# Hybrid GLA / state-space trunk: how the state-space preparation is stored, loaded and ranked

## The chip, the core and the metric

The kernel runs on one core of a Trainium2 chip. The metric is the device time of one execution in microseconds (us), the median of several runs. Engines are named as in the profile: PE is the matrix engine (PEld its weight loads), DVE the vector engine, ACT the scalar engine, POOL GpSimd, SP the engine from whose queue most transfers are issued.

## What is computed

A sequence of 512 tokens of width 1024 goes through two layers and a final norm. Layer 0 is gated linear attention with four heads, layer 1 a state-space mixer with 128 groups of 64 complex states:

```python
for i in range(DEPTH):                        # DEPTH = 2
    if i % 2 == 0:
        h = _rmsnorm(x, gla_norm[j])
        out = _gla_mixer(h, gla_w_in[j], gla_w_gate_up[j], gla_b_gate[j], gla_head_gain[j], gla_w_out[j])
    else:
        h = _rmsnorm(x, s5_norm[j])
        out = _s5_mixer(h, s5_w_in[j], s5_lam_re[j], s5_lam_im[j], s5_log_dt[j], s5_b_re[j], s5_b_im[j],
                        s5_c_re[j], s5_c_im[j], s5_d[j], s5_w_glu[j], s5_b_glu[j], s5_w_out[j])
    x = x + out
return _rmsnorm(x, final_norm)

# in _s5_mixer: what depends on parameters alone
dt = jnp.exp(log_dt)[:, None]
lam_bar = jnp.exp(lam * dt)
b_bar = ((lam_bar - 1.0) / lam)[..., None] * b_cplx
# and the recurrence that it is needed for: state <- lam_bar * state + b_bar u, y = Re(C state) + d u
```

## The kernel before, in words

The program is unrolled. Every instruction is traced in program order, and a scheduler then writes a fixed order for each engine ahead of time: it simulates the engines, and whenever one is free it takes, of the instructions whose inputs are there, the one with the lowest priority number. That number counts up with each traced instruction. `later(n)` adds n to it for a block, so that the block ranks as if it had been traced n instructions later. On the chip each engine then works through its written order, and an instruction whose input is late holds up all that stand behind it on that engine.

Layer 0 runs head by head (h = 0 to 3). A head projects v (`proj_v`), q and k (`proj_qk`) and z (`proj_z`), does the attention in four token blocks (`Attn.scores`, `state`, `mix`), and turns its output by PE transposes (`turn`). The output projection of a head (`proj_out`) is run inside the next head, between `proj_v` and `proj_z`. Weights come in units of 128 x 1024 (`wunit`): one load to `wraw` from SP's queue (L175), a cast to a high half on ACT (L158 or L180), and the low half by a DVE subtraction (L159) or by an accumulating transfer from POOL's queue (L181, L182). A matmul takes three passes, high by high, high by low, low by high. `proj_v` leaves its result in the four PSUM banks `pd`, and its evacuation `ev` (ACT L161, DVE L162) has to empty them before `proj_out` can use them.

The state-space layer needs matrices that depend on parameters alone. `S5Prep` builds them beside layer 0. Its `small` part is a generator in steps, one for a `tick()` in head 0: exponentials, sines, powers of lam_bar. Its fourth step makes the powers on POOL, its fifth transposes them on PE and stores them: `lpt` in 16 transfers of 32 KB (L1221), `pw` in four (L1224). `zero()` stores zero pads in `kz`, with 16 transfers of 56 KB from one tile (L957); it is called after head 0's `weave`. From head 1 on, `hook()` takes steps from a list, `plan`, at a rate (`RATES`) for each unit of the main work:

- F, for 16 blocks: `finish_b` of the block before, `compute` (eleven DVE operations, L1283 to L1301), `load` of the next block (four transfers, L1267 to L1273). The first F also loads block 0.
- Z: `finish_z`, which stores the rest, makes a convolution kernel on PE, and writes it to `kz`.
- E, for 8 tables: `etab`, six forms of DVE operation on 512 columns, twelve operations for two tables (L1251 to L1256), and four stores of 256 KB each (L1259). Its input `et` is made on POOL in the third step of `small`.
- G: `gcopy`, a rearranging copy.

`LOWS` gives what `later` adds for each kind of step. The first entries of `plan` are F0, E0, E1, F1, Z1, E2. All steps carry `issue_after(mark[...])`: they stand behind the last weight unit on each engine. The pools that matter here are `q4` (9 buffers of 4 KB a partition) and `tmp` (4 buffers of 2 KB).

The lines that the change and the prediction touch:

Of the kernel before, what the change touches and what calls it, by code (L numbers as in the profile page):

```python
# [9 lines left out]
F32 = mybir.dt.float32  # L10
# [11 lines left out]
P = 128  # L22
# [37 lines left out]
USP = 50  # L60
SEQ0 = 'h0 u h2 u h4 u s h6 u x0 t x1 q0 q1 t'
GP = 4
RATES = [0.84, 0.84, 0.88, 0.94, 0.94]
LOWS = {'F': 30, 'Z': 30, 'E': 100, 'G': 0}
ETABS = [2, 3, 3, 3, 3, 3, 3, 3, 4, 4, 4, 4, 4, 4, 4, 7, 8]
POS = [[0, 0, 1, 2, 1, 2, 3, 1, 2, 3, 3], [0, 1, 1, 3, 4, 5, 6, 5, 5, 7, 9], [0, 1, 3, 4, 4, 5, 6, 5, 6, 8, 8], [1,
    1, 4, 4, 4, 5, 6, 6, 6, 6, 8], [0, 0, 0, 0]]
# [20 lines left out]
def trunk_kernel(  # L88
# [5 lines left out]
    nc = tc.nc  # L94
    V, A, G, S, PE = nc.vector, nc.scalar, nc.gpsimd, nc.sync, nc.tensor
# [19 lines left out]
    def PT():  # L115
        return PS_("pt", 2)
# [19 lines left out]
    def tmp(dt=F32):  # L136
        return T_([P, 512], "tmp", 4, dt)
# [16 lines left out]
    mark = {}  # L154
# [169 lines left out]
    prep = S5Prep(tc, dr, C_, T_, PT, ident, q4, q2, big, tmp, s_bi, s_xc)  # L324
# [4 lines left out]
    @contextmanager  # L329
    def later(n):  # L330
        tc.cur_priority += n
        yield
        tc.cur_priority -= n

    def pinned(fn):
        with ExitStack() as es_:
            for k in ("pe", "act", "dve", "sp"):
                es_.enter_context(tc.issue_after(mark[k]))
            fn()

    def tick():
        if prep.t in SMALL:
            with later(LOW1):
                pinned(lambda: next(sm, None))
        prep.t += 1

    plan = []
    ne = 0
    for cb in range(NB + 1):
        plan.append(("F", cb))  # L350
        if cb:
# [8 lines left out]
    def hook():  # L360
        pace[0] += RATES[phase[0]]
        while pace[0] >= 1:
            pace[0] -= 1
            if plan:
                st = plan.pop(0)
                with later(LOWS[st[0]]):
                    prep.step(mark, *st)
# [41 lines left out]
    def proj_r():  # L409
        raw = tmp()[:, :P].rearrange("p (k n) -> p k n", n=16)  # L410
        hi = tmp(F32R)[:, :P].rearrange("p (k n) -> p k n", n=16)
        lo = tmp(F32R)[:, :P].rearrange("p (k n) -> p k n", n=16)
        S.dma_start(out=raw, in_=w_r.rearrange("p (k n) -> p k n", n=16))
        split(hi, lo, raw)
        acc = PT()
        for kb in range(8):
            three(acc[:16, :], hi[:, kb, :], lo[:, kb, :], hh[kb], hl[kb], kb == 0, kb == 7, True)
        V.tensor_tensor(out=rT, in0=acc[:16, :], in1=rbc[:16, :], op=MUL)
# [116 lines left out]
    def weave(gens, toks):  # L535
        i = 0
        for gen in gens:
            for _ in gen:
                with later(SCP):
                    for p, fn, b in toks:  # L540
                        if p == i:
                            fn(b)
                if prep.t < TOFF:
                    if i % 2:
                        tick()
                else:
                    hook()
                i += 1
# [79 lines left out]
    for h in range(NH):  # L628
        v = ([], [])
        box = []  # L630
        o = ([], [])
        trn = turn(box, o)
        if h == 0:
            v = v0
            proj_r()
        phase[0] = h - 1 if h else 0
        gt = nxt.pop() if nxt else gate(h)
        if h > 0:
            ptrn(0)
            ptrn(1)  # L640
        qk = proj_qk(h, gt[1], gt[2])
        if h > 0:
            ptrn(2)
            ptrn(3)
        if h == 0:
            tick()
        else:
            for _ in range(QZ[0]):
                hook()
        at_ = Attn(gt[0], qk, v, box)  # L650
        z = proj_z(h, box)
        tk = toks(h, at_)
        if h < 3 and GP >> h & 1:
            tk.append((GPOS[h], lambda b: nxt.append(gate(b)), h + 1))
        if h == 0:
            weave([z], tk)
            prep.zero()
            tick()
        elif h < NH - 1:
            weave([proj_v(h, *v), proj_out(h - 1, prev, range(2)), z], tk)  # L660
        else:
            weave([proj_v(h, *v), proj_out(h - 1, prev, range(1)), z], tk)
            weave([proj_out(h - 1, prev, (1,))], [(POS[4][b], trn, b) for b in range(4)])
            load_a(0)
            load_b(0)
        prev, ptrn = o, trn
# [20 lines left out]
    pt = PT()  # L687
# [194 lines left out]
    w = win()  # L882
# [22 lines left out]
    for tb in range(NT):  # L905
        for k in range(2):
            S.dma_start(out=f(x1p)[k * 64:(k + 1) * 64, 2 * tb:2 * tb + 2].rearrange("p q d -> p (q d)"),
                        in_=x1d.rearrange("(c j) d -> j c d", j=T)[2 * tb + k])
# [21 lines left out]
class S5Prep:  # L930
# [21 lines left out]
    def zero(self):  # L952
        zero = self.tmp()[:, :112]
        self.nc.gpsimd.memset(zero, 0.0)
        kzf = self.kz.bitcast(F32).rearrange("g i w -> (g i) w")
        for k in range(16):
            self.nc.sync.dma_start(out=kzf[k * P:(k + 1) * P, 0:112], in_=zero)  # L957

    def C2(self, shape, tag, dt=F32):
        return self.T_(shape, tag, 1, dt)  # L960
# [1 line left out]
    def small(self, lam_re, lam_im, log_dt, s_d):  # L962
        nc = self.nc
        V, A, G, PE = nc.vector, nc.scalar, nc.gpsimd, nc.tensor
# [56 lines left out]
        for q in range(4):  # L1021
            xt = self.q4().rearrange("p (g k w) -> p g k w", g=16, k=2)
            for k in range(2):
                g0 = k * 64 + q * 16
                nc.sync.dma_start(out=xt[k * 64:(k + 1) * 64].rearrange("p g k w -> p (g k w)"),
                                  in_=self.s_xc[0:64, g0:g0 + 16, :].rearrange("p g w -> p (g w)"))
# [29 lines left out]
        E, em1 = pexp(ar)  # L1056
# [115 lines left out]
        pt = self.PT()  # L1172
# [12 lines left out]
        pt = self.PT()  # L1185
# [26 lines left out]
        for ri, src in enumerate((LR, LI)):  # L1212
            for q in range(2):
                pt = self.PT()
                for k in range(4):
                    PE.transpose(pt[:64, k * P:(k + 1) * P], src[:, :, 4 * q + k], self.ident)
                ev = h2k()[:64].rearrange("g (a b c) -> g a b c", a=4, b=2)
                V.tensor_copy(out=ev.rearrange("g a b c -> g (a b c)"), in_=pt[:64, :])
                for k in range(4):
                    jp = 7 - (4 * q + k)  # L1220
                    nc.sync.dma_start(out=self.lpt[jp, :, ri].rearrange("(q g) p -> g q p", q=2), in_=ev[:, k])  # L1221
        for ri, src in enumerate((pc, pd)):
            for k in range(2):
                nc.sync.dma_start(out=self.pw[ri * 64:(ri + 1) * 64, k * 64:(k + 1) * 64, :].rearrange("p g t -> p (g t)"),  # L1224
                                  in_=src[k * 64:(k + 1) * 64].rearrange("p g k t -> p (g k t)"))
# [116 lines left out]
    def step(self, mark, code, cb):  # L1342
        with ExitStack() as st:
            for k in ("pe", "act", "dve", "sp"):
                st.enter_context(self.tc.issue_after(mark[k]))
            if code == "F":
                if cb:
                    self.finish_b(cb - 1)
                else:
                    self.load(0)  # L1350
                if cb < NB:
                    self.compute(cb)
                if cb + 1 < NB:
                    self.load(cb + 1)
            elif code == "Z":
                self.finish_z(cb - 1)
                if cb >= 2:
                    self.gcopy(cb - 2)
            elif code == "G":
                self.gcopy(cb)  # L1360
            else:
                self.etab(cb)
# [56 lines left out]
```

## Time and profile before

| | before |
|---|---|
| median of 3 runs | 1044.32 us (1040.68 to 1048.78) |
| profiled execution | 1042.2 us |
| its span, first to last instruction | 1040.5 us |
| mean granted PE clock | 0.943 of 2.4 GHz |
| PE busy | 921.3 us (89%) |
| DVE busy | 715.5 us (69%) |
| ACT busy | 471.4 us (45%) |
| POOL busy | 101.2 us (10%) |
| DMA | 205.79 MB, 198 GB/s over the span |

Shares are of the span. A busy PE is not a PE at its peak, and the average hides stages with different limits, so the stages are read one by one below. An engine's wait is put down to what came last by the profile.

### The profile page before, as it was taken

The page shows a single profiled execution, that of the slowest core. Times are in us where ns is not written, and L with a number is a line of the kernel's source. Part 1 is how long each engine was busy: PE and PEld are TensorE (multiplying, and loading weights), DVE is VectorE, ACT ScalarE, POOL GpSimd, SP SyncE. Part 2 cuts the span into 40 slices and gives each one's busy share as a digit, 9 for nine tenths or more (in the row PEclk, how much of TensorE's full clock was granted, in tenths as well). Part 3 has the DMA queues.
Part 4 walks back from the last instruction along what each step waited for, and adds up shares of the span by engine and source line. Part 5 has one row for each costly group of instructions (what it writes and reads, how often), then busy time and mean ns, then how long its engine had stood idle before and what let it go on. Part 6 is the DMA issues. An engine that isn't in the chain of part 4 may idle for free. (4 is left out here: it accounts for less than half of the span.)

```text
span 1040.5 us, 13590 instructions
## 1 busy us (share of the span) xinstructions
PE 921.3 (89%) x5019; PEld 715.9 (69%) x5019; DVE 715.5 (69%) x1225; ACT 471.4 (45%) x707; POOL 101.2 (10%) x168
## 2 busy tenths in 40 slices
PE   6895961899969984989999979999999999999996
PEld 5573750676747763767777768787778888888885
DVE  5793559977899768988947758798998542424322
ACT  5553342436546643543666573743443532313212
POOL 4175700002001200000100000000000000000000
PEclk9997985799979987999999989999999999999998
DMA  8884376899979999899684526777766432252312
GB/s 258 233 180 99 69 203 196 233 263 286 295 229 246 287 284 288 235 281 312 214 247 171 182 92 218 249 263 254 237 186 200 128 102 83 99 170 93 101 61 81
DMA packets 118707, 205.79 MB, mean 198 GB/s; under 512 B 32400, under 2 KB 69824, under 8 KB 118640
## 3 DMA queue, kind: packets, MB, share of 16 engines
q1 hardware_dynamic: 110208, 180.90, 54.9%
q0 software_dynamic: 5472, 19.02, 9.9%
q10 hardware_dynamic: 2960, 4.99, 1.4%
q8 instruction: 39, 0.64, 0.2%
q14 instruction: 28, 0.23, 0.1%
HBM read 167.69 MB, written 45.59 MB: 205 GB/s over the span
## 5 line engine op out<-in xcount | busy, mean ns | idle before, releaser
L159 DVE TENSOR_TENSOR whl<-wraw,whl 128x1024 fp32r<-128x1024 f32 x100 | 122.0, 1222 | 156.5 <-ACT whl L158 156.2
L158 ACT CAST whl<-wraw 128x1024 fp32r<-128x1024 f32 x100 | 104.9, 1049 | 191.1 <-PE pd L194 50.2
L193 PE MATMUL pd<-whl,actA 128*128 128x512 f32 x384 | 152.9, 404 | 13.3 <-ACT whl L158 9.0
L194 PE MATMUL pd<-whl,actA 128*128 128x512 f32 x384 | 153.0, 398 | 0.0
L195 PE MATMUL pd<-whl,actA 128*128 128x512 f32 x384 | 151.4, 399 | 0.0
L189 PE MATMUL pd<-actA,whl 128*128 128x512 f32 x256 | 102.3, 406 | 7.3 <-ACT u L723 6.2
L191 PE MATMUL pd<-actA,whl 128*128 128x512 f32 x256 | 101.4, 397 | 0.0
L193 PEld LDWEIGHTS pd<-whl,actA 128*128 128x128 f32 x384 | 73.1, 191 | 32.4 <-ACT whl L158 9.0
L195 PEld LDWEIGHTS pd<-whl,actA 128*128 128x128 f32 x384 | 72.9, 190 | 17.6 <-issue 2.4
L194 PEld LDWEIGHTS pd<-whl,actA 128*128 128x128 f32 x384 | 73.1, 190 | 16.9 <-issue 1.2
L193 PE MATMUL pd<-whl,q 128*128 128x512 f32 x192 | 79.0, 412 | 4.4 <-DVE tmp L387 2.7
L194 PE MATMUL pd<-whl,q 128*128 128x512 f32 x192 | 77.9, 406 | 0.0
L180 ACT CAST whl<-wraw 128x1024 fp32r<-128x1024 f32 x36 | 37.7, 1047 | 74.7 <-PE pd L194 32.2
L189 PEld LDWEIGHTS pd<-actA,whl 128*128 128x128 f32 x256 | 48.6, 190 | 19.8 <-ACT u L723 7.2
L191 PEld LDWEIGHTS pd<-actA,whl 128*128 128x128 f32 x256 | 48.7, 190 | 11.3
L189 PE MATMUL po<-actA,whl 128*128 128x512 f32 x128 | 51.7, 404 | 3.8 <-ACT whl L180 3.8
L190 PE MATMUL pd<-actA,whl 128*128 128x512 f32 x128 | 52.1, 407 | 0.0
L191 PE MATMUL po<-actA,whl 128*128 128x512 f32 x128 | 50.4, 396 | 1.3 <-DMA whl<-w_qk 1.3
L195 PE MATMUL pd<-whl,q 128*128 128x512 f32 x128 | 50.9, 409 | 0.0
L723 ACT ACTIVATE u<-pd,rsP 64x256 f32<-64x256 f32 x64 | 48.2, 753 | 3.5 <-DVE mxr L716 2.6
L190 PE MATMUL pd<-big,whl 128*128 128x512 f32 x120 | 47.6, 398 | 1.1 <-DVE big L159 1.1
L193 PEld LDWEIGHTS pd<-whl,q 128*128 128x128 f32 x192 | 37.3, 194 | 15.4 <-DVE tmp L387 3.1
(327 smaller groups left out, 2001.2 us busy)
## 6 DMA issues: line engine op xcount, KB each, us to landing
wraw<-w_glu SPq DMA_DIRECT2D x32, 512.0 KB, 3.5
wraw<-w_v SPq DMA_DIRECT2D x16, 512.0 KB, 4.7
wraw<-w_z SPq DMA_DIRECT2D x16, 512.0 KB, 6.7
whl<-w_z POOLq DMA_DIRECT2D x16, 512.0 KB, 7.9
q<-lpt SPq DMA_DIRECT2D x16, 512.0 KB, 6.8
q<-s_bi SPq DMA_DIRECT2D x16, 512.0 KB, 8.5
wraw<-w_out SPq DMA_DIRECT2D x16, 512.0 KB, 5.5
bmd<-q SPq DMA_DIRECT2D x16, 512.0 KB, 5.1
```

The source lines that it names most:

```text
L158: i0 = A.copy(out=dst_hi, in_=src)
L159: i1 = V.tensor_tensor(out=dst_lo, in0=src, in1=f(dst_hi), op=SUB)
L180: A.copy(out=hi, in_=raw)
L189: PE.matmul(acc, lhsT=wh, rhs=ah, start=first, stop=False)
L190: PE.matmul(acc, lhsT=wh, rhs=al, start=False, stop=False)
L191: mark["pe"] = PE.matmul(acc, lhsT=wl, rhs=ah, start=False, stop=last).ins
L193: PE.matmul(acc, lhsT=ah, rhs=wh, start=first, stop=False)
L194: PE.matmul(acc, lhsT=ah, rhs=wl, start=False, stop=False)
L195: mark["pe"] = PE.matmul(acc, lhsT=al, rhs=wh, start=False, stop=last).ins
L723: A.activation(out=dst, in_=src, func=AF.Copy, scale=rsP[hs, tb:tb + 1])
```

## The change

Five edits, all in the preparation:

- `zero()` is called early, after `proj_r()` of head 0, and writes all pads with one transfer instead of 16. The source is one tile of zeros, read 16 times.
- `lpt` is stored with 4 transfers instead of 16, each with four powers; the transposes are put in reverse order for it.
- The load of block 0 is a step of its own, L, taken right after the last `tick()` of head 0 with no `later`. Before, it was the first thing of F0.
- The first two tables, E0 and E1, are taken out of the list that head 1 starts, and are run in head 0's `weave`, at its even units.
- `LOWS`: F and Z go from 30 to 150, E from 100 to 200.

```diff
 GP = 4
+EARLY = 2
 RATES = [0.84, 0.84, 0.88, 0.94, 0.94]
-LOWS = {'F': 30, 'Z': 30, 'E': 100, 'G': 0}
+LOWS = {'F': 150, 'Z': 150, 'E': 200, 'G': 0}
...
-    plan = []
-    ne = 0
+    plan = [("E", k) for k in range(EARLY)]
+    ne = EARLY
     for cb in range(NB + 1):
         plan.append(("F", cb))
...
                 if prep.t < TOFF:
                     if i % 2:
                         tick()
+                    elif plan[0][0] == "E":
+                        with later(LOWS["E"]):
+                            prep.step(mark, *plan.pop(0))
                 else:
                     hook()
...
             v = v0
             proj_r()
+            prep.zero()
...
             weave([z], tk)
-            prep.zero()
             tick()
+            prep.step(mark, "L", 0)
...
         zero = self.tmp()[:, :112]
         self.nc.gpsimd.memset(zero, 0.0)
-        kzf = self.kz.bitcast(F32).rearrange("g i w -> (g i) w")
-        for k in range(16):
-            self.nc.sync.dma_start(out=kzf[k * P:(k + 1) * P, 0:112], in_=zero)
+        kzf = self.kz.bitcast(F32).rearrange("g i w -> (g i) w").rearrange("(k p) w -> p k w", p=P)
+        self.nc.sync.dma_start(out=kzf[:, :, 0:112], in_=zero.unsqueeze(1).to_broadcast([P, 16, 112]))
...
                 for k in range(4):
-                    PE.transpose(pt[:64, k * P:(k + 1) * P], src[:, :, 4 * q + k], self.ident)
+                    PE.transpose(pt[:64, k * P:(k + 1) * P], src[:, :, 4 * q + 3 - k], self.ident)
                 ev = h2k()[:64].rearrange("g (a b c) -> g a b c", a=4, b=2)
                 V.tensor_copy(out=ev.rearrange("g a b c -> g (a b c)"), in_=pt[:64, :])
-                for k in range(4):
-                    jp = 7 - (4 * q + k)
-                    nc.sync.dma_start(out=self.lpt[jp, :, ri].rearrange("(q g) p -> g q p", q=2), in_=ev[:, k])
+                nc.sync.dma_start(out=self.lpt[4 - 4 * q:8 - 4 * q, :, ri].rearrange("j (q g) p -> g j q p", q=2), in_=ev)
...
             if code == "F":
                 if cb:
                     self.finish_b(cb - 1)
-                else:
-                    self.load(0)
                 if cb < NB:
                     self.compute(cb)
...
+            elif code == "L":
+                self.load(cb)
             elif code == "G":
                 self.gcopy(cb)
```

## Rows read from the trace of the kernel before

**Rows 1.** Busy time by stage: window, length, busy (and count), clock, DMA share, GB/s.

```profile
140.00:340.00 200.00, 153.28 (x656) 113.22 (x654) 175.55 (x319) 96.13 (x150) 14.15 (x15) 0.85 0.88 249
340.00:500.00 160.00, 139.40 (x615) 106.13 (x614) 129.20 (x244) 77.33 (x128) 11.70 (x12) 0.91 0.93 276
500.00:620.00 120.00, 108.99 (x735) 85.98 (x734) 82.31 (x139) 76.64 (x111) 3.20 (x7) 0.97 0.58 187
```

**Rows 2.** The same view of shorter stretches; order PE, PEld, DVE, ACT, POOL.

```profile
40.00:80.00 40.00, 38.00 (x163) 26.90 (x163) 34.68 (x83) 21.72 (x29) 22.88 (x41) 0.99 0.87 197
...
146.10:188.70 42.60, 7.60 (x28) 3.76 (x26) 37.65 (x69) 12.64 (x22) 0.00 (x0) 0.55 0.75 230
285.90:301.80 15.90, 7.21 (x40) 3.67 (x39) 15.53 (x43) 6.75 (x15) 0.00 (x0) 0.63 0.54 177
399.70:418.90 19.20, 5.70 (x29) 2.92 (x27) 16.82 (x38) 9.55 (x19) 1.73 (x2) 0.57 0.96 261
190.00:300.00 110.00, 98.28 (x429) 73.60 (x428) 91.28 (x167) 56.33 (x87) 10.69 (x11) 0.93 0.91 259
```

**Rows 3.** Timeline of PE around the first gap: start, duration, instruction, idle before.

```profile
146.13 0.40 PE L195 MATMUL pd<-whl,actA 128*128 128x512 f32 x1
...
188.70 0.79 PE L193 MATMUL pd<-whl,q 128*128 128x512 f32 x1 [1.43 <-DVE big L162]
```

**Rows 4.** Timeline of DVE in the first gap.

```profile
151.75 1.22 DVE L1283 TENSOR_TENSOR q<-q,q 128x1024 f32<-128x1024 f32 x1 [4.91 <-DMA q<-s_bi]
...
164.07 0.29 DVE L488 COPY_PREDICATED att<-cmask,pt 128x128 f32<-128x128 uint8 x1
...
171.62 0.21 DVE L167 CAST big<-att 128x128 fp32r<-128x128 f32 x1
...
187.90 1.40 DVE L162 SCALAR_TENSOR_TENSOR big<-pd,rstd,big 128x512 fp32r<-128x512 f32 x2
```

**Rows 5.** Busy time of DVE from 146.1 to 188.7: first L162, then L159.

```profile
146.10:188.70 42.60, 3.63 (x11) 0.55 0.75 230
...
146.10:188.70 42.60, 5.85 (x8) 0.55 0.75 230
```

**Rows 6.** Timeline of SP's queue, 119 to 148: start, time until the last issue.

```profile
119.10 2.99 SPq L957 DMA_DIRECT2D kz<-tmp  x6
123.25 12.69 SPq L1221 DMA_DIRECT2D lpt<-q  x16
136.04 2.91 SPq L1224 DMA_DIRECT2D pw<-q  x4
138.99 5.84 SPq L957 DMA_DIRECT2D kz<-tmp  x10
144.88 0.58 SPq L1267 DMA_DIRECT2D q<-lpt  x1
...
146.88 0.85 SPq L175 DMA_DIRECT2D wraw<-w_out  x2
```

**Rows 7.** DMA issues: transfer, queue, count, KB each, median us to landing.

```profile
kz<-tmp SPq DMA_DIRECT2D x16, 56.0 KB, 1.6
lpt<-q SPq DMA_DIRECT2D x16, 32.0 KB, 2.1
```

**Rows 8.** Groups of DVE operations by form, 146 to 190: one of a table's six.

```profile
L1251 DVE TENSOR_TENSOR q<-big,big 128x512 f32<-128x512 f32 x3 | 2.0, 680 | 0.0
```

**Rows 9.** Timeline of DVE in head 0.

```profile
101.83 0.33 DVE L1331 TENSOR_TENSOR dk<-dm,kd 128x16 f32<-128x16 f32 x1 [9.71 <-DMA kd<-kdd]
...
114.81 0.17 DVE L260 TENSOR_SCALAR rv<-ssq 128x4 f32<-128x4 f32 x1 [6.97 <-ACT tmp L265]
```

**Rows 10.** Timeline of POOL: the last operation on the tables' input.

```profile
108.43 0.73 POOL L984 TENSOR_TENSOR big<-q,q 128x256 f32<-128x256 f32 x1
```

**Rows 11.** One tile's instructions (tab): count, duration ns min/median/max, first and last start.

```profile
L1259 SPq DMA_DIRECT2D tab<-q x32: 452/654/1544, 177.7 to 539.0; - x32
L572 SPq DMA_DIRECT2D q<-tab x13: 319/383/660, 543.3 to 752.5; - x13
```

## The prediction, written before the change was run

> **What bounds the kernel now.** I read the busy times by stage first, then PE's idle stretches, then the order of DVE, SP and POOL inside the largest. After 620 us PE is nearly full, so a change of the preparation has to earn its time before that. From 140 to 340 us PE is busy 153.3 of 200 and DVE 175.6; from 340 to 500 PE 139.4 of 160 and DVE 129.2, with the DMA engines at 0.93 [rows 1]. So layer 0 has two engines near their limit in turn, and PE loses 67 us there.
>
> Three stretches hold most of the loss, each at the same place of a head: between the last matmul of `proj_v` and the first of `proj_out`. In head 1 PE is busy 7.60 of 42.6 us, so 35.0 are idle; in head 2 it idles 8.7 of 15.9, in head 3 13.5 of 19.2 [rows 2]. The first runs from 146.13 to 188.70, and what releases PE is DVE's L162 on the PSUM banks `pd` [rows 3]: the evacuation of v, which could have begun at 146.5, starts on DVE at 187.90 [rows 4]. DVE is not idle meanwhile: 37.65 of 42.6 us [rows 2]. Of this the main work is 3.63 us of L162 and 5.85 of L159 [rows 5], and some 2 us of the attention's L488 and L167, four of each at 0.29 and 0.21 [rows 4]: 11.5 us. The other 26 us are preparation. Its effect is plain in one pair: L167 needs nothing but L488, ended at 164.4, and starts at 171.62 [rows 4]. In between stand steps whose rank is ahead of v's evacuation: F0 is traced before the weave, E0, E1 and F1 in its first units, and 30 or 100 instructions are about one or three units of 24 matmuls and their casts.
>
> In front of this stands a wait: DVE's L1283, first operation of F0, waits 4.91 us for block 0's load [rows 4]. The load was late for SP's queue: from 119.10 to 144.83 it issues pads, `lpt`, `pw` and pads again, and only then the load, with the weights of `proj_out` behind it at 146.88 [rows 6].
>
> **The change part by part.** The terms are made against the profiled execution, 1042.2 us (span 1040.5 and 1.7 around it). The median of the runs is 1044.3, so 2.1 are added at the end.
>
> *Priorities.* With 150 in place of 30, F0 ranks some five units of main work later, F1 and Z1 likewise, so all of v's evacuation and of head 1's attention ranks ahead of them. What does not change is that an engine with nothing better ready takes a preparation step. So the gap closes to something between two ends. Least: the main chain alone, 3.63 us of L162 and one weight split of 5.85 / 8 or up to 1.2, so about 5 us idle. Most: all 11.5 us of main work and one preparation operation of 1.22 (L1283's 1.22 [rows 4]) in front of each of the eleven L162, 13.4 more: 25 us. I take 13, a little below the middle, since by then ACT's half (L161) is also freed of its preparation. Gain **22** (10 to 30).
>
> *Clock.* In that gap the granted clock was 0.55 [rows 2], near the lower of the two levels, after PE had idled. The 7.60 us of matmuls would be 4.2 at full clock. A shorter gap gives part of it back: gain **2** (0 to 3.4).
>
> *Heads 2 and 3.* Their gaps show the same pattern at 8.7 and 13.5 us of idle PE, with DVE busy 15.53 of 15.9 and 16.82 of 19.2 [rows 2]. Here the change brings rank alone, and the preparation pushed out of head 1 arrives just then. Gain **5** (0 to 16).
>
> *Where the work goes.* Of the 26 us of preparation, twelve table operations of 0.68 [rows 8] are 8.2 us and are moved to head 0. Some 18 us move later. From 190 to 300 DVE has 110 − 91.3 = 18.7 us free, and from 500 to 620 another 37.7 [rows 1, 2]. They fit, barely in the first, and PE will sometimes wait: cost **4** (0 to 18). The last table store is issued at 539.0 and the first of the later table loads at 543.3 [rows 11]; that pair is not the same table, and the list now starts two steps shorter, so I take nothing for it. If the tables came later than their readers, each would be a wait of a few us in the state-space stage.
>
> *Fewer issues.* Sixteen `lpt` stores take 12.69 us of SP's queue, 0.79 each, and sixteen pads 8.83 [rows 6]. Four and one at the same price each leave 3.2 and 0.6: SP is free some 17 us sooner, less the eight table stores that come in, at 0.65 [rows 11] some 5. So block 0's load and the weights behind it are issued about 12 us sooner, near 133, and the 4.91 us wait in front of the gap is gone. I do not count that twice: it lies in the 35 us. A single store of four powers may be dearer to issue than one of a power; up to four times as dear, nothing is gained on `lpt`, and the load still comes 3 us sooner.
>
> Here the Trainium skill speaks against the change. Its page "DMA: Bandwidth & Descriptors", section "Issuing engines are not separate DMA queues", says that what is saved on the issuing sequencer is usually small beside the transfer itself. This trace does not agree for these stores: 0.79 us each to issue [rows 6] against 2.1 us to landing [rows 7], and the landings overlap while the issues do not. By the rule the 4.91 us wait would stay, and the sum would be 1028; by the row it is the 1023 below.
>
> *Early pads.* The same 0.92 MB now go out in the stage around 40 to 80 us, where PE is busy 38.0 of 40 and the DMA engines 0.87 at 197 GB/s [rows 2]. At that rate they take 4.7 us of all engines. Hidden wholly they cost nothing, and the later stage gains a little; in front of weights they cost all. The pads were never in anyone's way as data, only as issues, 1.6 us each to landing [rows 7]. Cost **2** (−1 to 4.7). Behind SP's wait for the zeros stand the weight loads; behind POOL's memset the accumulating weight transfers. The tile holds one of four `tmp` buffers until the transfer has landed; `gate` wants three, `small` has one, so `gate`'s third waits for its second operation, which comes before it anyway.
>
> *Tables in head 0.* Their input is ready on POOL at 109.2 [rows 10], and DVE then waits for ACT until 114.81, 6.97 us in all [rows 9]. The 8.2 us of tables fit for the larger part. Behind them on DVE stand L260 and the evacuation of z, which PE's next `proj_v` waits for. Cost **2** (0 to 15.6, the upper end below).
>
> Sum: −22 − 2 − 5 + 4 + 2 + 2 = −21, so 1021.2 for an execution like the profiled one, and **1023** for the median.
>
> **The rivals.**
>
> *Rank changes little.* The written order is mostly set by what is ready, and preparation still fills each hole of the chain. Then only the wait of 4.91 and the 8.2 us of tables leave the gap: −13 + 4 = −9, **1035**. For it: DVE has no idle time in the gap after 152. Against it: L167 stood 7 us behind an L488 that it alone needed, which is rank and not readiness.
>
> *The displaced work binds.* The 18 us fill DVE from 190 to 300 to 109 of 110, PE waits there for all of it, and heads 2 and 3 gain nothing: −22 − 2 + 18 + 4 = −2, **1042**. For it: DVE's 175.6 of 200 and DMA at 0.93 [rows 1]. Against it: the free 37.7 us after 500, to which work may now slide.
>
> *Slower: a table heads DVE's queue in head 0.* The scheduler may think `et` ready sooner than it is, and write E0 into DVE's order ahead of the attention of head 0. It did that with L1331, which held DVE for 9.71 us until 101.83 [rows 9] for a load. E0 would hold it until 109.2 [rows 10], 7.4 us more, and run 8.2: 15.6 us for all of head 0's chain. The scale `kap`, which the powers and so the load of block 0 need, stands behind it too, so F0's wait and the first gap stay as they were: 1044.3 + 15.6 − 2 = **1058**. It decides if E0 stands in DVE's order before that scale. For it: L1331. Against it: E ranks 200 later, and POOL's chain is long in any model.
>
> *All three gaps close.* −30 − 3 − 15 + 0 + 2 + 2 = −44, **1000**. For it: one cause in all three. Against it: DVE and DMA in heads 2 and 3.
>
> **How the numbers follow.** A measurement of this kernel tells a change from none at about 1%, or 10 us: its three runs lie 8 us apart. Chances: forecast (1009 to 1034) 0.56, all three gaps 0.12, rank changes little 0.13, displaced work binds 0.08, slower 0.11. Faster by over 1% is below 1033.9: the forecast nearly whole, the three gaps and a third of the rank rival, 0.70. Slower by over 1% is 0.11 and the rest, 0.19, lies within. The range from 998 to 1046 leaves out the slower rival, part of the full closing and the upper side of the binding one, about 0.18.
>
> **What would show it.** Right: in SP's queue four `lpt` stores and one pad, and block 0's load issued before 138; no wait of DVE for `s_bi` before the first gap; v's evacuation on DVE within 5 us of the last matmul of head 1's `proj_v`, the gap below 20 us; E0 on DVE between 107 and 125; DVE from 190 to 300 busier than 91 of 110. Wrong: a wait of DVE on POOL near 100 us; the gap still over 30; weights late between 45 and 70; new idle time of PE from 190 to 340 as long as what the gap gave. The prediction fails on size if the fillers in the main chain are other than the one for each step or two that I took.

## The result and the profile after

The changed kernel takes **1092.64 us** (median of 4 runs, 1089.03 to 1096.49) against 1043.01 for the kernel before in the same session: ratio **1.0472**, 95% interval 1.0439 to 1.0505. It is slower by 50 us. The forecast of 1023 had the wrong sign, its range ended at 1046, and its slowest rival stood at 1058. The profiled execution has a span of 1092.0 us, 51.5 more than before. Two single executions took far longer than the others of their kernels, 2109.6 us in `b_early` below and 1268.53 in the kernel before beside it; the medians and ratios here leave them out.

Where it is lost shows in the starts of a few matmuls on PE's timeline (us):

| first matmul of | before | after | difference |
|---|---|---|---|
| `proj_out` of head 0, in head 1 (end of the first gap) | 188.7 | 209.6 | +20.9 |
| `proj_out` of head 1, in head 2 | 301.8 | 331.9 | +30.1 |
| `proj_out` of head 2, in head 3 | 418.9 | 462.8 | +43.9 |
| the state-space layer | 506.3 | 554.2 | +47.9 |
| end of the span | 1040.5 | 1092.0 | +51.5 |

So 21 us are lost before the end of the gap that was to shrink, 23 more by `proj_out` in head 3, and 8 after that. By stage (columns as in [rows 1]):

```profile
140.00:340.00 200.00, 149.91 (x636) 111.30 (x635) 160.44 (x292) 92.11 (x146) 13.10 (x14) 0.83 0.80 223
340.00:500.00 160.00, 131.86 (x559) 98.54 (x559) 118.96 (x216) 72.44 (x107) 14.19 (x15) 0.88 0.84 231
500.00:620.00 120.00, 108.83 (x550) 84.23 (x549) 79.37 (x142) 60.41 (x101) 2.56 (x7) 0.96 0.69 225
```

From 140 to 500 PE and DVE are both less busy than before [rows 1], by 11 and 25 us: less gets done in the same time.

The stretches of idle PE, the first being the gap that answers to the one of 42.6 us [rows 2]:

```profile
170.30:209.60 39.30, 6.88 (x26) 3.67 (x25) 38.32 (x68) 14.00 (x26) 0.00 (x0) 0.55 0.59 187
320.60:331.90 11.30, 7.78 (x37) 3.37 (x37) 11.23 (x39) 5.65 (x13) 0.00 (x0) 0.50 0.54 162
404.00:414.70 10.70, 0.95 (x9) 0.07 (x5) 9.40 (x17) 6.48 (x9) 1.74 (x2) 0.50 1.05 270
456.50:462.80 6.30, 5.80 (x28) 3.20 (x29) 5.85 (x23) 3.14 (x8) 0.00 (x0) 0.50 0.18 51
```

The first gap is 39.3 us long with DVE busy 38.3 of it: it has only moved. The third stretch, 404 to 414.7, in front of head 3's `proj_v`, answers to a wait of 1.87 us in the kernel before; it has DMA at 1.05 and DVE at 9.4 of 10.7.

Head 0 lost the most at one place. DVE's timeline, then PE's (lines stand 1 to 4 higher than before: L507 is the state update that was L506, L1253 to L1258 are a table's six operations, and L988 is POOL's work on their input, which was L984):

```profile
112.53 0.69 DVE L1253 TENSOR_TENSOR q<-big,big 128x512 f32<-128x512 f32 x1 [5.08 <-POOL big L988]
113.14 1.14 DVE L1256 TENSOR_TENSOR q<-big,big 128x512 f32<-128x512 f32 x1
115.62 0.69 DVE L1254 TENSOR_TENSOR tmp<-big,big 128x512 f32<-128x512 f32 x1 [1.34 <-POOL big L988]
116.35 1.45 DVE L1255 TENSOR_TENSOR q<-q,tmp 128x512 f32<-128x512 f32 x1
117.72 0.74 DVE L507 SCALAR_TENSOR_TENSOR big<-po,ges,tmp 128x512 f32<-128x512 f32 x1
```

```profile
118.51 0.80 PE L194 MATMUL po<-big,big 128*128 128x512 f32 x1 [20.38 <-DVE big L507]
```

DVE waits 5.08 us for POOL with a table's first operation, runs four of its six, and only then updates the attention's state. PE stands still for 20.38 us; in the kernel before the wait at this place was 6.86:

```profile
100.87 0.80 PE L193 MATMUL po<-big,big 128*128 128x512 f32 x1 [6.86 <-ACT big L520]
```

SP's queue after (as in [rows 6]):

```profile
122.21 3.07 SPq L1261 DMA_DIRECT2D tab<-q  x4
...
138.47 1.31 SPq L1223 DMA_DIRECT2D lpt<-q  x2
...
144.95 1.48 SPq L1223 DMA_DIRECT2D lpt<-q  x2
...
153.38 0.57 SPq L1269 DMA_DIRECT2D q<-lpt  x1
```

The four stores of powers are cheap to issue, about 0.7 us each as a single one was. But they begin 15 us later than the sixteen did, at 138.47 and not 123.25, and block 0's load is issued at 153.38, not "before 138": 144.88 was the time before [rows 6].

### The profile page after: what moved, and what is told of

It reads as the page before. It is cut to its first block, busy times and chain, and to the rows that moved or that the text cites. A ratio compares the mean times of both kernels' runs of the same rounds, so it can differ in the third digit from the quotient of the medians.

```text
span 1092.0 us, 13543 instructions
## 1 busy us (share of the span) xinstructions
PE 935.2 (86%) x5019; PEld 725.0 (66%) x5019; DVE 720.4 (66%) x1225; ACT 472.7 (43%) x707; POOL 101.9 (9%) x168
## 4 chain that ended last, share of the span: by engine, by line
PE 50%; DMA 20%; DVE 16%; ACT 8%; issue 3%; SPq 1%; POOL 1%; ACTq 0%; POOLq 0%; DVEq 0%
PE pd L194 6%; PE pd L195 6%; PE pd L196 6%; PE pd L191 5%; PE pd L190 5%; PE pd L192 5%; DMA wraw<-w_z 4%; ACT u L728 3%; DMA cmd<-q 3%; DMA kz<-kf 2%; DMA q<-s_bi 2%; PE po L191 2%; PE po L190 2%; PE po L192 2%; DVE q L1310 2%
## 5 line engine op out<-in xcount | busy, mean ns | idle before, releaser
L159 ACT CAST whl<-wraw 128x1024 fp32r<-128x1024 f32 x100 | 104.9, 1049 | 198.6 <-PE pd L195 61.3
L194 PEld LDWEIGHTS pd<-whl,actA 128*128 128x128 f32 x384 | 74.2, 193 | 43.1 <-DVE tmp L388 10.6
L196 PEld LDWEIGHTS pd<-whl,actA 128*128 128x128 f32 x384 | 74.0, 193 | 17.5 <-issue 1.6
L195 PEld LDWEIGHTS pd<-whl,actA 128*128 128x128 f32 x384 | 74.1, 193 | 16.2 <-issue 0.8
L181 ACT CAST whl<-wraw 128x1024 fp32r<-128x1024 f32 x36 | 37.7, 1046 | 80.8 <-PE pd L195 32.8
L190 PEld LDWEIGHTS pd<-actA,whl 128*128 128x128 f32 x256 | 49.1, 192 | 20.9 <-ACT u L728 7.1
L1325 PE MATMUL pt<-q,bh 128*32 128x256 f32 x128 | 21.9, 496 | 34.8 <-DVE q L163 24.8
```

What stands on the lines that cost most here:

```text
L159: i0 = A.copy(out=dst_hi, in_=src)
L181: A.copy(out=hi, in_=raw)
L190: PE.matmul(acc, lhsT=wh, rhs=ah, start=first, stop=False)
L194: PE.matmul(acc, lhsT=ah, rhs=wh, start=first, stop=False)
L195: PE.matmul(acc, lhsT=ah, rhs=wl, start=False, stop=False)
L196: mark["pe"] = PE.matmul(acc, lhsT=al, rhs=wh, start=False, stop=last).ins
```

## The experiments

Each kernel is compared with the kernel before on the same chip; the ratio has its 95% interval. Kernels whose name begins with b are the kernel before with one part of the change or another small edit.

### The parts one by one

**The tables alone** (`b_early`): `EARLY = 2`, the two tables out of head 1's list, and the branch in `weave`, nothing else. 1056.95 us, ratio 1.011 [1.0061, 1.0158].

> The kernel before with one part of the change alone: E0 and E1 moved into head 0. Theory (the two tables cost head 0 its chain: the state's own operations stand behind them): first matmul of head 1's qk later by 15 to 20 us and the end with it, 1058 to 1063. First rival (the tables only fill holes of DVE, and the late head 0 of the changed kernel came from the pads): 1040 to 1046. Second rival (the loss in head 0 is there but the 8.2 us that leave the gap of head 1 give half of it back): 1050 to 1055.

The same kernel once more, with the trace that is read here (`b_early2`): 1057.46, ratio 1.0146 [1.0106, 1.0187].

> The kernel before with the two tables in head 0 alone, once more, because the profiled execution of the first time took 2108 us and cannot be read. Time 1053 to 1061 as there. Theory (the tables' second operand takes a buffer of tmp, so the state's decay waits for one and stands behind the tables): the first state update L507 of head 0 runs after the four DVE operations of E0, past 112 us, and PE is idle 15 to 20 us there; some 5 us are given back in the gap of head 1. Rival (head 0 is as before, and the loss arises later): PE idle 6.9 us there as before.

The theory holds, but for the 5 us to be given back. PE, then DVE (L1255 is a table's first operation in this kernel):

```profile
113.94 0.80 PE L194 MATMUL po<-big,big 128*128 128x512 f32 x1 [20.12 <-DVE big L507]
```

```profile
107.97 0.69 DVE L1255 TENSOR_TENSOR q<-big,big 128x512 f32<-128x512 f32 x1 [5.39 <-POOL big L988]
...
113.15 0.74 DVE L507 SCALAR_TENSOR_TENSOR big<-po,ges,tmp 128x512 f32<-128x512 f32 x1
```

PE is 13 us later there than at 100.87 in the kernel before, and the first gap ends 11.5 us late, at 200.2, so under 2 us are given back.

**The changed kernel without them** (`a_noearly`): `EARLY = 0`. 1075.60, ratio 1.0295 [1.023, 1.0359]: 17 us of the 50 go.

> The changed kernel with no tables in head 0, all else of the change kept. Theory (tables cost 19 us in head 0, pads 5): 1092.6 - 19 = 1074, with head 1's first qk near 112. Rival (the loss in heads 2 and 3 hangs on the tables too, because they shift what is prepared when): below 1060. Rival (the tables were not the cause): 1088 to 1096.

The theory holds: 1075.60 for its 1074, and head 1's first matmul of q and k comes at 112.26.

**Why the state stands behind the table** (`b_early_u`):

```diff
-        u = self.tmp().rearrange(...)
+        u = (self.q4()[:, 0:512] if ck < 2 else self.tmp()).rearrange(...)
```

> The two tables in head 0 alone, with the second operand of these two in a buffer of q4 in place of tmp. Theory (the buffer, not the place in head 0, costs the time): the state's decay and update keep their place, head 0 is as before, 1036 to 1046. Rival (eight DVE operations and a POOL chain at this place cost head 0 in any buffer): 1053 to 1061 as with tmp.

1057.63, ratio 1.0136 [1.0084, 1.0187]. Half right. Head 0 is nearly as before: the state update comes at 105.07, ahead of the table, and the first gap ends at 187.0 (188.7 before).

```profile
103.24 0.80 PE L194 MATMUL po<-big,big 128*128 128x512 f32 x1 [8.11 <-ACT big L521]
```

```profile
105.07 0.74 DVE L507 SCALAR_TENSOR_TENSOR big<-po,ges,tmp 128x512 f32<-128x512 f32 x1
...
108.78 0.69 DVE L1255 TENSOR_TENSOR q<-big,big 128x512 f32<-128x512 f32 x1 [1.36 <-POOL big L988]
```

So the buffer is what puts the state behind the table: the decay of the state is written to a `tmp` tile (four buffers), the two tables hold two of them, and a scheduler that finds no buffer for the decay fills DVE with the table (the last step is read from the kernel, not measured). But the total did not improve. Most of what head 0 no longer loses is lost between 187 and 312: `proj_out` of head 1 begins at 311.9, 10.1 us late (15.0 with the loss in head 0, 316.8), and the state-space layer at 521.9, 15.6 late (525.8).

**The priorities alone** (`b_low`): `LOWS` 150, 150, 200. 1060.57, ratio 1.0148 [1.0106, 1.0189].

> The kernel before with the lower priorities alone. My forecast's term: the gap from 146 to 188 closes to about 18 us, heads 2 and 3 give some more, 1015 to 1025. Rival (preparation is picked as a filler whatever its rank, so the order stays): the gap stays 40 to 43 us, 1040 to 1046. Rival (work pushed out of head 1 arrives in heads 2 and 3, where the changed kernel lost 14 us in front of head 3's proj_v): 1055 to 1068.

Both rivals' mechanisms at once, with the second's time: the first gap stays, and heads 2 and 3 lose.

```profile
145.00:186.90 41.90, 7.18 (x25) 3.75 (x25) 36.86 (x66) 12.04 (x20) 0.00 (x0) 0.54 0.77 229
```

In DVE's written order 64 operations stand from F0's first one to the first evacuation of v, 39 of them preparation, in the kernel before and with the lower priorities alike; in the changed kernel it is 41 of 80. The first loss is in front of head 3's `proj_v`, PE and DVE:

```profile
383.09 0.80 PE L193 MATMUL pd<-whl,actA 128*128 128x512 f32 x1 [9.71 <-DVE tmp L387]
```

```profile
376.41 1.23 DVE L1283 TENSOR_TENSOR q<-q,q 128x1024 f32<-128x1024 f32 x1 [5.60 <-DMA cmd<-q]
...
382.36 0.68 DVE L387 SCALAR_TENSOR_TENSOR tmp<-tmp,pd 128x512 f32<-128x512 f32 x1
```

DVE waits 5.60 us with a preparation step, by the profile for the landing of a store (`cmd` out of a `q4` tile). It then runs eight preparation operations and two of the main work until 382, and only then L387, which PE waits for. The kernel before has the same step at 369.05 with a wait of 4.68 (for a load), but L387 is next behind it, and PE waits 1.87. DVE, then PE before:

```profile
369.05 1.22 DVE L1283 TENSOR_TENSOR q<-q,q 128x1024 f32<-128x1024 f32 x1 [4.68 <-DMA q<-s_bi]
370.19 0.68 DVE L387 SCALAR_TENSOR_TENSOR tmp<-tmp,pd 128x512 f32<-128x512 f32 x1
```

```profile
370.93 0.51 PE L193 MATMUL pd<-whl,actA 128*128 128x512 f32 x1 [1.87 <-DVE tmp L387]
```

At `proj_out` of head 3 this kernel is 6.0 us late (424.9), at the state-space layer 14.7 (521.1). In between PE waits for DVE with a preparation step of its own, which the kernel before does not:

```profile
476.53 1.08 PE L1323 MATMUL pt<-q,bh 128*32 128x256 f32 x8 [6.26 <-DVE bh L1301]
```

Which steps (`b_lowfz`, F and Z at 150, E at 100): 1061.60, ratio 1.0157 [1.0119, 1.0195]. All of it is F and Z.

> The kernel before with F and Z at 150 and the tables E at 100 as before. If the 16 us lost by the lower priorities come from F and Z (their loads and operations fall later into heads 2 and 3, where the DMA engines are busy all the time): 1053 to 1063. If they come from the tables at 200: 1040 to 1047.

The other direction (`b_hi`, F and Z at 0): 1046.45, ratio 1.0022 [0.9998, 1.0047], between the two theories. Its first gap ends at 189.3: rank doesn't move it from this side either.

> The kernel before with the opposite of the change's priorities: F and Z at 0 in place of 30, E at 100 as before. Theory (lower priority only pushes preparation into heads 2 and 3, so a higher one draws it forward): 1030 to 1042, proj_out of head 3 earlier than 466. Rival (the rank of 30 is a balance, and main work is delayed by a higher one): 1048 to 1070.

A control (`b_31`, F and Z at 31): 1041.22, ratio 0.9954 [0.9928, 0.998]. A few rows exchanged in the written order move the time by half a per cent; parts that lose 1.5% are not explained by that, and of those that lose 0.5 to 0.8% it can be a share. DVE's order is that of the kernel before up to 370 us, yet the first gap ends at 191.4 (188.7) and `proj_out` in head 2 begins at 303.9 (301.8): differences under 3 us between the starts of two single executions say nothing.

> The kernel before with the rank of F and Z at 31 in place of 30, which moves some ten DVE instructions near 370 us by a few places and nothing else of DVE. A control: if a new written order by itself costs the 8 to 15 us that every single part lost in heads 2 and 3, it is 1046 to 1058. If these losses have causes of their own: 1040 to 1046.

**The pads** (`b_pads`, one transfer, early): 1053.69, ratio 1.0075 [1.0049, 1.01]. The same transfer at the old place (`b_pads_inplace`): 1050.04, ratio 1.005 [1.0027, 1.0073].

> The kernel before with the pads alone: one transfer, issued before the weave of head 0. Theory (it delays the weights of z in a stage where PE is busy 38.0 of 40): 5 us lost by 80 us and kept to the end, 1048. Rival (the loss is given back, because SP's queue is free of 16 issues before block 0's load): 1040 to 1045. Forecast's term was +2.

> The kernel before with the pads as one transfer of 896 KB at the old place alone. If it is the cause of the 12 us lost by the three parts on SP's queue together: 1050 to 1057. If not: 1038 to 1046; beside it, the early place of the same transfer lost 8 us, so the same time as there would say that the single transfer costs and not its place.

By the medians 6 of 9 us are the form and 3 the early place (the intervals overlap). The theory for `b_pads` (1048) is short by nearly 6 us. The early loss is where it was looked for: with the pads in front of the weights PE waits 4.03 us at 73.47 for DVE's L461, where the kernel before has no wait of 1.5 us between 40 and 80. The other loss was not expected. DVE at the old place, and the lines that answer to it in the kernel before:

```profile
146.84 1.23 DVE L1282 TENSOR_TENSOR q<-q,q 128x1024 f32<-128x1024 f32 x1 [5.01 <-DMA q<-s_bi]
147.99 0.68 DVE L445 TENSOR_TENSOR big<-big,u 128x512 f32<-128x512 f32 x1
...
150.31 0.68 DVE L460 SCALAR_TENSOR_TENSOR big<-po,big 128x512 f32<-128x512 f32 x1
```

```profile
142.72 0.69 DVE L445 TENSOR_TENSOR big<-big,u 128x512 f32<-128x512 f32 x1 [0.44 <-ACT big L443]
...
143.93 0.68 DVE L460 SCALAR_TENSOR_TENSOR big<-po,big 128x512 f32<-128x512 f32 x1
...
151.75 1.22 DVE L1283 TENSOR_TENSOR q<-q,q 128x1024 f32<-128x1024 f32 x1 [4.91 <-DMA q<-s_bi]
```

With ten fewer issues in the queue block 0's load comes 6.4 us sooner, at 138.49. In the written order F0 now stands in front of head 1's gate (L445) and scaling (L460). The data still comes 5 us later than DVE gets there. The wait has not gone: it was behind the main chain's operations and is now ahead of them. `b_pads` has the same order, with a wait of 5.87 us at 150.56.

**Stores and load.** Four stores of the powers (`b_lpt`): 1046.96, ratio 0.9991 [0.9964, 1.0017]. The load as its own step (`b_load`): 1053.14, ratio 1.0081 [1.0054, 1.0107]. Both, with the single pad transfer at its old place (`b_store`): 1054.37, ratio 1.0122 [1.0085, 1.0158].

> The kernel before with the powers stored by 4 transfers alone (the pads 16 transfers, the first load inside F0 as before). If these stores free the queue by 9 us: load issued near 136, 1038 to 1042. If the loss of 12 us of the three parts together comes from them (a landing of 3.4 us for four powers, waited for): 1050 to 1057. If it comes from the load as a step of its own or the single pad transfer: 1040 to 1046.

> The kernel before with block 0's load as a step of its own at the end of head 0 alone. The three parts on SP's queue together lost 12 us and the stores of the powers alone lost none. If the load step is the cause (it holds q4 and big buffers and DMA time sooner, in front of weights): 1050 to 1057. If the single pad transfer is: 1040 to 1046.

> The kernel before with the parts that only shorten SP's queue: four transfers for the powers, the first load a step of its own, the pads one transfer at the old place. My forecast's term: SP is free 12 to 17 us sooner, block 0's load is issued before 138 (144.88 before), the DVE wait of 4.91 us is gone, 1035 to 1041. Rival (the load waits for the landing of the powers and not for the queue, and gap 1 is DVE's preparation work anyway): 1041 to 1047, load not before 142. Rival (a transfer of four powers is dearer to land than four single ones): over 1048, load after 148.

The stores do what they should and it is worth nothing (1046.96 lies just above the range that `b_lpt` has for that): four issues take 2.95 us of the queue, not 12.69 [rows 6], and the load goes out at 140.91. In `b_lpt` DVE no longer waits for it at all. But two casts of `proj_out`'s weights now stand in front of head 1's gate on ACT, and the first waits for its load. ACT, then DVE:

```profile
144.06 1.05 ACT L158 CAST whl<-wraw 128x1024 fp32r<-128x1024 f32 x1 [6.46 <-DMA wraw<-w_out]
```

```profile
150.06 0.69 DVE L445 TENSOR_TENSOR big<-big,u 128x512 f32<-128x512 f32 x1 [0.82 <-ACT big L443]
```

The gate comes 7.3 us later than at 142.72: here too a wait has moved in front of the main chain. In `b_store` DVE's wait for the load falls from 4.91 [rows 4] to 1.27,

```profile
149.78 1.23 DVE L1281 TENSOR_TENSOR q<-q,q 128x1024 f32<-128x1024 f32 x1 [1.27 <-DMA q<-s_bi]
```

and the gap still ends at 189.0. None of the three expectations for `b_store` has this pair, an earlier load and a later end. The load as its own step (`b_load`, 1053.14 as the first expectation has it) is issued later, at 148.12, since the pads now stand in front of it; the first gap ends sooner, at 180.3, with 25 preparation operations of 44 in front of v's evacuation, and the 8 us are given back by 305.5 (301.8 before).

### Closing the gap in another way

If rank does not move F0, place does (`b_pace4`): the counter that paces the preparation begins lower, so F0 is traced behind the last unit of `proj_v`, and E0, E1 and F1 behind v's evacuation.

```diff
-    pace = [0.0]
+    pace = [-4.0]
```

In `b_pace4r` the rates are also raised, and `b_pace2r` is half the shift.

> The kernel before with the preparation's pace counter begun at -4 in place of 0: F0, E0, E1, F1 are traced about five units later, past v's evacuation, with priorities as before. Theory (in the gap of head 1 it is the place where preparation is traced, and not its rank, that sets DVE's order): the gap from 146 to 188 falls to 18 to 28 us, proj_out begins at 165 to 175; what is displaced costs 5 to 15 in heads 2 and 3; end 1025 to 1043. Rival (the first gap is the main chain's own and its loads'): the gap stays over 38 and the end is 1045 to 1060.

> As the one with the counter at -4, and the rates of preparation per unit raised from 0.84, 0.88, 0.94 to 0.90, 0.96, 0.98, so that the later steps stand about where they stood. If the displaced work costs by coming late: 5 to 10 us less than with the counter alone. If it costs by its density in heads 2 and 3: the same or 5 us more.

> The kernel before with the pace counter begun at -2 and the rates at 0.88, 0.93, 0.97. With -4, 23 us won in the gap of head 1 were all given back by 520 us. If the preparation as a whole is what the layer waits for, wherever it lies: gap about 30, end 1042 to 1052. If half the shift costs less than half the return: 1025 to 1038.

The first theory has the gap right (169.4) and the end wrong (1055.11, the rival's):

| kernel | first gap ends | `proj_out` in head 2 | in head 3 | state-space layer | span | ratio |
|---|---|---|---|---|---|---|
| before | 188.7 | 301.8 | 418.9 | 506.3 | 1040.5 | 1 |
| `b_pace4` | 169.4 | 288.4 | 410.1 | 514.5 | 1055.0 | 1.0082 [1.0053, 1.0111] |
| `b_pace4r` | 165.6 | 289.2 | 413.3 | 508.7 | 1048.8 | 1.0059 [1.0033, 1.0085] |
| `b_pace2r` | 170.3 | 296.5 | 416.3 | 517.1 | 1053.4 | 1.0096 [1.007, 1.0122] |

The gap does close, with 6 preparation operations of 30 where 39 of 64 stood. A later place moves two things, the rank of a step and the weight unit behind which `issue_after` puts it. Lower ranks alone moved nothing in the gap (`b_low`), so the unit is the likelier cause, but no run moved it alone. Windows of `b_pace4r`, the first gap and two later ones:

```profile
143.90:165.60 21.70, 5.30 (x18) 3.60 (x17) 15.07 (x36) 8.97 (x19) 0.00 (x0) 0.55 0.74 227
260.00:289.20 29.20, 15.94 (x69) 10.41 (x67) 27.89 (x57) 13.96 (x26) 0.00 (x0) 0.68 0.85 254
388.40:413.30 24.90, 5.75 (x29) 3.15 (x29) 20.73 (x43) 12.53 (x23) 1.73 (x2) 0.57 1.00 284
```

23.1 us are won at the first, 12.6 are left at head 2's `proj_out`, 5.6 at head 3's, and none at the state-space layer (one execution each). The idle time comes up again at the same place of the next heads. Half the shift closes as much (170.3) and ends at 1054.53, above both of its expectations, so the return isn't in proportion to the shift. Raising the rates gives 6 us of span, but 1.6 of the medians (1055.11 and 1053.47), between its two expectations.

**Is it the amount of DVE work?** `b_less` and `b_pace4r_less` leave three of `compute`'s ten operations out for every block.

> The kernel before with three of the preparation's DVE operations left out for every block: the second and third product of B (0.68 us each) and the second product of z (1.22 us), 2.58 us a block, 41 us of DVE between 140 and 506. The state-space constants are then other ones. If DVE's amount of work is what layer 0 waits for: 15 to 35 us less, 1009 to 1029. If it waits for chains and loads, and the amount matters little: 1036 to 1046.

> The kernel with the pace counter at -4 and raised rates, with the same three operations left out for every block. If the gain of 23 us in head 1 was given back because the displaced work fills DVE later: this one keeps more of it, 20 us or more below the same kernel without the cut (1053) and below the cut kernel before. If it was given back for another reason (loads, the chain of the attention): it stands above the cut kernel before by 5 to 10 us again.

1037.68, ratio 0.9933 [0.9903, 0.9962], and 1035.39, ratio 0.9904 [0.9871, 0.9936]. The second theory of the first run is right: 41 us of DVE work less are worth 7. The waits in front of the preparation's operations grow meanwhile. Groups of DVE operations from 140 to 508, the kernel before and then `b_less`:

```profile
L1283 DVE TENSOR_TENSOR q<-q,q 128x1024 f32<-128x1024 f32 x16 | 19.5, 1220 | 27.0 <-DMA q<-s_bi 26.0 <-DVE tmp L429 1.0
L1292 DVE TENSOR_TENSOR q<-big,pp 128x1024 f32<-128x1024 f32 x16 | 19.5, 1219 | 13.0 <-DMA big<-s_xc 7.9 <-DMA wraw<-w_out 3.5 <-DMA pp<-pw 1.6
```

```profile
L1283 DVE TENSOR_TENSOR q<-q,q 128x1024 f32<-128x1024 f32 x16 | 19.6, 1224 | 30.4 <-DMA q<-s_bi 26.2 <-DMA cmd<-q 2.7 <-DMA tab<-q 1.5
L1290 DVE TENSOR_TENSOR q<-big,pp 128x1024 f32<-128x1024 f32 x16 | 19.6, 1223 | 18.1 <-DMA big<-s_xc 17.9
```

The last number before the releasers is the idle time in front: 40.0 us for these two lines, then 48.5. With the cut, the shift is worth some 2 us by the medians instead of costing 8 (1053.47 without the cut), which is between the two expectations (the intervals of the two kernels overlap). What its first gap gave (167.7 against 184.7) is given back all the same in the profiled execution, which is 5 us above its kernel's median: the state-space layer begins at 502.5 against 500.7. So the amount of DVE work is a part of the return (about 10 us of 31 by the medians), and not the whole.

## Why the prediction was wrong

**The step that failed first** is "With 150 in place of 30, F0 ranks some five units of main work later ... so all of v's evacuation and of head 1's attention ranks ahead of them", from which the gain of 22 was taken. Shown wrong: the order of DVE in the gap did not change, 39 of 64 both times, and the gap stayed at 41.9 us.

The count in that step is wrong for F0. Between F0 and v's evacuation 207 instructions are traced: 112 of `proj_v`'s four units, 25 of the attention, and 70 of the preparation's own steps, which the five units left out. So with 150 F0 still ranks 57 ahead of the evacuation. E0, E1, F1 and Z1 did fall behind it in rank, and their operations stayed where they were. Even in the kernel before, the first operation of F2, which is traced and ranked behind the evacuation, stands ahead of its start at 187.90 [rows 4]:

```profile
185.30 1.21 DVE L1283 TENSOR_TENSOR q<-q,q 128x1024 f32<-128x1024 f32 x1
```

The prediction's pair, L167 7 us behind the L488 that it alone needed, was read as rank. The argument "rank and not readiness" left out that the written order comes from simulated times: at the time when the scheduler filled those places L167 need not have been ready, and a filler is taken whatever its rank. (The simulated times are argued; the unchanged order and the filler of lower rank are shown.) The rival "rank changes little" had this part right, and its 0.13 was too little.

"Could have begun at 146.5" was a misreading too. DVE's half of the evacuation (L162) needs ACT's (L161), and ACT came to it at 185.32, behind two preparation steps that waited. ACT's timeline before:

```profile
182.50 0.37 ACT L1327 ACTIVATE tmp<-pt,par 128x128 f32<-128x128 f32 x1 [3.75 <-PE pt L1323]
184.37 1.04 ACT L1307 CAST q<-q 128x1024 f16<-128x1024 f32 x1 [1.50 <-DMA tab<-q]
185.32 2.42 ACT L161 ACTIVATE big<-pd,rstd 128x512 fp32r<-128x512 f32 x4
```

**The second step** is that a closed gap is a gain. `b_pace4r` closed it by as much as was forecast (22, 10 to 30: 23.1 us), and it ended 8 us slower. "Where the work goes", put at 4 (0 to 18), measured 31 in that kernel. It was costed as DVE time that fits into DVE's free time. What shows in the later heads of `b_low` is other: a preparation step that waits for a transfer stands in front of a main operation (376.41 above). The DMA engines were at 0.91 from 190 to 300 and at 0.93 from 340 to 500 already [rows 1, 2], and 40 us of DVE's idle time are waits in front of the two preparation lines above. The prediction named the DMA share and priced no such wait. That the transfers of layer 0 bind it fits all of this, but no run took bytes away, so it stays argued. The cause of the loss of `b_early_u` between 187 and 312 stays open.

**Terms, as forecast and as measured alone:**

| term | forecast | measured |
|---|---|---|
| priorities, with clock, heads 2 and 3, displaced work | −25 | +16.2 (`b_low`) |
| tables in head 0 | +2 (0 to 15.6) | +12.6 and +15.0 |
| pads as one early transfer | +2 (−1 to 4.7) | +9.3 |
| four stores of the powers | inside the 22 | +1.5 (0.9991: none) |
| load as its own step | 0 | +9.2 |

These are differences of medians. The ratios add up to 4.4% (1.48, 1.46 of `b_early2`, 0.75, -0.09, 0.81), and the change measured 4.7% (4.4 to 5.05): within the intervals the parts add up.

*Clock.* The granted clock in the first gap stayed at 0.55, so the 2 us were not gained.

*Tables.* The slower rival had the right price, 15.6 at most, and the right engine, but not its condition: it was to decide "if E0 stands in DVE's order before that scale" `kap`. What it stood before is the attention's state, and by way of a buffer; the wait for POOL came with it. The prediction counted `tmp` buffers for the pads and not for the tables.

*Pads.* The upper bound of 4.7 held for the early stage (4.03 at 73.47). What was missing is that an earlier load lets F0 be written ahead of head 1's gate.

*Fewer issues.* The estimate for the stores was right (2.95 us for 3.2), the one for the load was not: in `b_store`, which has all three parts, it was issued 3.3 us sooner (141.57) and not 12. In the changed kernel it went the other way, since everything on PE and DVE came 20 us later. The page of the Trainium skill that the prediction weighed ("DMA: Bandwidth & Descriptors", section "Issuing engines are not separate DMA queues") has the time on the issuing sequencer as usually small beside the transfer. The row had spoken against it (0.79 against 2.1 us), but what was saved was worth nothing here (ratio 0.9991 in `b_lpt`), even with DVE's wait down from 4.91 to 1.27 in `b_store`.

*Signs.* E0 was to come between 107 and 125 and came at 112.53. DVE from 190 to 300 was to be busier than 91 of 110 and was busy 87.0. Of the notes under "Wrong", the wait of DVE on POOL near 100 us is the 5.08 us above, and the gap "still over 30" is 39.3.

No kernel with a gain worth having was found: `b_31` at 0.9954 beats the kernel before by half a per cent, with a reordering of a few rows for which no reason can be given beforehand.

## What to carry to other kernels

A long idle stretch of PE with another engine full of side work is a reservoir, not a loss: before counting it as gain, find the next place where that side work must go, and price there its waits for loads as well as its busy time. In a list-scheduled kernel a lower priority need not move a step, for a scheduler with an idle engine takes what is ready. Count what is traced in between, the side work's own instructions with it, move where the step is traced, and compare the written order before believing that anything moved. For each new step count the buffers it takes from every pool: two tiles of a pool of four put the main chain behind a table, and an earlier load moved a wait of 5 us from behind the main chain to the front of it.

## Unexpected in the hardware

The tables took longer in head 0 than their 0.68 us an operation [rows 8], while POOL was at work on SBUF. DVE of `b_early_u`, beside POOL and then after it, and POOL's last long operations (L1255, L1258 and L1259 are operations of a table, L388 is the evacuation of z):

```profile
121.71 0.67 DVE L388 SCALAR_TENSOR_TENSOR tmp<-tmp,pd 128x512 f32<-128x512 f32 x1
...
123.42 1.57 DVE L1255 TENSOR_TENSOR q<-big,big 128x512 f32<-128x512 f32 x1
124.91 1.57 DVE L1258 TENSOR_TENSOR q<-big,big 128x512 f32<-128x512 f32 x1
...
131.41 0.69 DVE L1259 TENSOR_TENSOR q<-big,big 128x512 f32<-128x512 f32 x1
```

```profile
121.40 1.55 POOL L988 TENSOR_TENSOR q<-q,q 128x512 f32<-128x512 f32 x1
122.91 3.02 POOL L988 TENSOR_TENSOR q<-q,big 128x512 f32<-128x512 f32 x2
```

The same shape takes 1.57 us beside POOL and 0.69 without, while L388, with one operand in PSUM, stays at 0.67 at 121.71 beside a POOL operation of 1.55. The Trainium skill's page "SBUF — State Buffer", section "SBUF: two separate sides", says that a VectorE operation with two SBUF inputs and a GpSimd operation that reads SBUF exclude each other for a whole instruction; these rows agree with it. The six operations of E0 took 7.1 us there and not 4.1, so the prediction's 8.2 us for two tables was short too.
